# Retention's gate as a transposed product, and one copy moved from ScalarE to VectorE

## The chip, the cores and the metric

One of the eight cores of a Trainium2 chip runs the whole program. The metric is the device time in microseconds of one execution, taken as the median of several runs. The five engines that appear below are TensorE (PE; its weight loads are shown apart, as PEld), VectorE (DVE), ScalarE (ACT), GpSimd (POOL) and SyncE (SP), which here issues nearly all transfers (DMAs). Each engine takes its instructions in the order in which the program emits them.

## The reference

One encoder layer over 1024 tokens of width 1024, all in float32. What matters here is the first half, up to the output projection:

```python
proj = h @ W_in            # split into retention q, k, v, gate; S5 input; attention q, k, v
y_ret = retention(...)     # 4 heads of 64; per head normalised, then multiplied by silu(gate)
y_ssm = s5_mixer(...)      # y = gelu(..); y * sigmoid(y @ w_glu + b_glu)
y_att = window_sink_attention(...)
mix = concatenate([y_ret, y_ssm, y_att]) @ W_out
h = LN(alpha*h + mix); h = LN(alpha*h + ExpertChoiceSwiGLU(h))   # 16 experts, 128 tokens each
```

The last step of retention is the one that is touched: `out = ((out - mu) * rsqrt(var + eps)).reshape(seq, 256)` and `silu(g) * out`, with `g = h @ W_in[:, 768:1024]`. In the state space part it is the turned copy of `y` that feeds the product with `w_glu`.

## The kernel before

Float32 products of full accuracy are made as three products of a split pair: each operand is kept as a high part and a low part (`whl`, `hT`, both of type fp32r), and `mm3` (lines 64 to 66) issues high by high, high by low and low by high. Splitting is a copy on ScalarE (the high part) and a subtraction on VectorE (the low part).

After the input norm the kernel works through a list of products over the projected columns. The order is written out by hand in `order` (line 1237), and each entry advances a place `s`; every piece of work is given a place with `at(place, fn)`, and `F.run()` emits all of it sorted by place. So the places decide the order on each engine's own queue, and on SP's; when an instruction runs is decided by what it waits for. Places below are given relative to `V0`, the place of the first entry.

The entries are:

- `q` (lines 1243 to 1258): attention's queries, eight products `qUH` (column unit U, token half H), transposed, that is columns by 512 tokens, 24 matmuls of 512 columns each in three parts. ScalarE copies the high part to `kst` (line 901), VectorE makes the low part from the same bank (line 936), and SP stores both to `q_d` with four DMAs (line 947).
- `g` (lines 1259 to 1264): retention's gate, one product for each of the eight chunks of 128 tokens, tokens by 256 columns, 24 matmuls of 256 columns in two parts, then Silu on ScalarE into a 256-wide tile (line 403).
- `r` (lines 1265 to 1277): a chunk of retention: scores (line 422) and their decay on VectorE (428), the output (434, 435), statistics on VectorE and GpSimd (442 to 448), the norm (453 on VectorE, 456 on ScalarE), multiplication by the gate on VectorE (460), two transposes on PE (466), a copy out of PSUM on ScalarE (473) and the store to `y_d` on SP (474). The last four stand 4, 6, 9 and 14 behind the output in place; for the last chunk closer.
- `V0 o0 K0 V1 K1`: attention's values and keys, and between them the first output product `o0` of the state space part, which reads what SP loaded into `MUW` (lines 837 to 841) and `Z` (848).

Beside these run other things on the same queues. On VectorE: the scan of the state space part (lines 716 to 719, 724 to 727) and its corrections (`fix`, 742 and 743). On ScalarE: the stores' preparation `SO` (753 to 755), whose last one stands at place 74.75. At place 75.7 `early_space` closes the scan's memory and opens another pool in it: GpSimd and VectorE make `rel` and `R` there (1432 to 1436), and SP issues `sink` and the first eight `MUW` loads; at 81.7 the two loads of `Z` for `o0`. `mat.load(0)` (line 960), the first megabyte of the output matrix, stands at the place of the entry `q30`. Eight small lag products (line 785) lie among the first entries, and their banks are emptied by ScalarE (794); they share two PSUM banks with the scores. The products of the list share two other banks.

After `K1` come the other three output products of the state space part, their turn (`turned`, lines 872 to 879: four copies `yT`, two on ScalarE and two on VectorE), the gate products with `w_glu` (884), attention and the output projection, placed by a table of numbers (`PLACES`, lines 1742 to 1797); then the 16 experts, which are matmuls on split weights loaded a megabyte at a time, from about 455 us to the end.

## Time and profile before

| | |
|---|---|
| median of 3 runs | 1563.07 us (1562.83 to 1563.98) |
| the profiled execution | 1562.62 us, its span 1560.9 us |
| mean granted clock of TensorE | 0.996 |
| busy share of the span | PE 99%, PEld 81%, DVE 90%, ACT 72%, POOL 12% |
| DMA | 507.20 MB, mean 325 GB/s |
| HBM read and written | 461.75 MB and 42.99 MB |

Times in the trace are microseconds from the start of the span. The profiled execution took 1.7 us more than its span. A row of the timeline has the start, the duration, the engine, the line, the operation, the tiles (written <- read) and the shape; in brackets stands the engine's idle time before it and what ended it. A row of the waits has the total, the number of times and the longest. A row of the windows has the busy time of each engine in a stretch, the clock, the share of the DMA engines' time and GB/s.

### The profile page before, as it was taken

What the parts mean: (1) busy time and instruction counts of PE and PEld (TensorE: products, weight loads), DVE (VectorE), ACT (ScalarE), POOL (GpSimd) and SP (SyncE); (2) the same over time, 40 slices, a digit from 0 to 9 for tenths busy, and PEclk for the clock granted to TensorE, in tenths of its full rate; (3) what the DMA queues carried; (4) which work ended last, traced back from release to release, by engine and by line L of the source; (5) the groups of instructions that cost most, each with busy time, mean ns of one, the idle gap of its engine ahead of it and who ended that gap; (6) DMA issues with size and microseconds to landing.
All of it is one profiled execution on the core that took longest, in us unless ns stands there. A gap on an engine that the chain in (4) does not pass through costs nothing.

```text
span 1560.9 us, 21150 instructions
## 1 busy us (share of the span) xinstructions
PE 1543.1 (99%) x7710; PEld 1262.5 (81%) x7710; DVE 1401.8 (90%) x1720; ACT 1130.7 (72%) x1329; POOL 191.5 (12%) x248
## 2 busy tenths in 40 slices
PE   9999999999999999999999999999999999999997
PEld 7887887888767888888888888888888888888886
DVE  7987965889989999999999999989999999999996
ACT  7746556887736777777777777787877878787773
POOL 4002111111010001010010101000211201021121
PEclk9999999999999999999999999999999999999999
DMA  6556478353179999999999999999999999999992
GB/s 242 185 167 155 119 232 234 102 166 109 72 311 371 373 390 411 427 387 367 392 371 387 371 401 370 403 411 409 421 412 409 415 425 413 417 414 413 402 415 108
DMA packets 105177, 507.20 MB, mean 325 GB/s; under 512 B 16752, under 2 KB 29808, under 8 KB 54640
## 3 DMA queue, kind: packets, MB, share of 16 engines
q1 hardware_dynamic: 88624, 474.81, 77.6%
q0 software_dynamic: 16304, 30.94, 7.2%
q8 instruction: 61, 1.00, 0.2%
q14 instruction: 44, 0.36, 0.1%
q10 hardware_dynamic: 144, 0.09, 0.0%
HBM read 461.75 MB, written 42.99 MB: 323 GB/s over the span
## 4 chain that ended last, share of the span: by engine, by line
PE 90%; ACT 3%; DMA 3%; DVE 2%; issue 1%; POOL 1%; SPq 1%; POOLq 0%; ACTq 0%; DVEq 0%
PE gu L2334 44%; PE y L2334 22%; PE mm L64 4%; PE mm L66 4%; PE mm L65 4%; PE tp L2317 3%; PE gu L2342 1%; PE po L1525 1%; PE tp L1505 1%; DMA wraw<-in_w_out 1%; PE at L1454 1%; PE sm L265 0%; DMA uT<-in_x 0%; ACT S L1497 0%; PE at L699 0%
## 5 line engine op out<-in xcount | busy, mean ns | idle before, releaser
L2426 DVE TENSOR_TENSOR whl<-wraw,whl 128x2048 fp32r<-128x2048 f32 x378 | 860.5, 2288 | 61.1 <-ACT whl L2417 57.1
L2417 ACT ACTIVATE whl<-wraw 128x2048 fp32r<-128x2048 f32 x378 | 725.3, 1919 | 246.3 <-PE gu L2334 132.5
L2334 PE MATMUL gu<-whl,xT 128*128 128x512 f32 x3000 | 712.5, 394 | 0.0
L2334 PEld LDWEIGHTS gu<-whl,xT 128*128 128x128 f32 x3000 | 555.4, 188 | 114.8 <-issue 1.0
L2334 PE MATMUL y<-whl,hT 128*128 128x512 f32 x1536 | 359.4, 389 | 0.0
L2334 PEld LDWEIGHTS y<-whl,hT 128*128 128x128 f32 x1536 | 288.0, 188 | 59.7
L2295 POOL DMA_INDIRECT xs<-h_d,index x15 | 26.7, 1777 | 451.3 <-PE y L2334 304.1
L64 PE MATMUL mm<-hT,whl 128*128 128x512 f32 x160 | 65.3, 408 | 0.0
L66 PE MATMUL mm<-hT,whl 128*128 128x512 f32 x160 | 62.6, 391 | 0.0
L65 PE MATMUL mm<-hT,whl 128*128 128x512 f32 x160 | 62.5, 391 | 0.0
L64 PE MATMUL mm<-WO,yh 128*128 128x512 f32 x128 | 53.4, 418 | 0.0
L56 DVE TENSOR_TENSOR hT<-tp,hT 128x512 fp32r<-128x512 f32 x76 | 51.5, 683 | 1.9 <-ACT hT L55 1.7
L55 ACT ACTIVATE hT<-tp 128x512 fp32r<-128x512 f32 x76 | 43.7, 581 | 12.8 <-PE tp L206 6.7
L66 PE MATMUL mm<-WO,yl 128*128 128x512 f32 x128 | 50.6, 396 | 0.0
L65 PE MATMUL mm<-WO,yh 128*128 128x512 f32 x128 | 50.6, 395 | 0.0
L2468 DVE TENSOR_TENSOR hid<-hid,gu 128x512 f32<-128x512 f32 x64 | 43.5, 680 | 2.0 <-PE gu L2334 2.0
L64 PE MATMUL mm<-whl,hT 128*128 128x256 f32 (+1 forms) x120 | 42.4, 353 | 1.5 <-ACT gate L403 1.5
L2462 ACT ACTIVATE hid<-gu 128x512 f32<-128x512 f32 x64 | 37.1, 580 | 5.7 <-PE gu L2342 5.5
L66 PE MATMUL mm<-whl,hT 128*128 128x256 f32 (+1 forms) x120 | 40.2, 335 | 0.0
L65 PE MATMUL mm<-whl,hT 128*128 128x256 f32 (+1 forms) x120 | 40.0, 333 | 0.0
L1465 DVE CUSTOM_DVE_ANT_0 S<-at,R,sink 128x384 f32<-128x384 f32 (+1 forms) x64 | 36.8, 577 | 2.3 <-PE at L1454 1.7
L2317 PEld LDWEIGHTS tp<-ident,hid 128*128 128x128 f32 x256 | 31.8, 140 | 8.5 <-issue 0.5
(450 smaller groups left out, 1779.4 us busy)
## 6 DMA issues: line engine op xcount, KB each, us to landing
wraw<-in_exp_w_up SPq DMA_DIRECT2D x128, 1024.0 KB, 9.5
wraw<-in_exp_w_down SPq DMA_DIRECT2D x128, 1024.0 KB, 10.2
wraw<-in_exp_w_gate SPq DMA_DIRECT2D x122, 1024.0 KB, 9.2
wraw<-in_w_in SPq DMA_DIRECT2D x6, 1024.0 KB, 5.3
whole<-in_exp_w_gate SPq DMA_DIRECT2D x6, 1024.0 KB, 8.5
q_d<-kst SPq DMA_DIRECT2D x32, 128.0 KB, 2.6
wraw<-in_w_out SPq DMA_DIRECT2D x4, 1024.0 KB, 7.6
qs<-q_d POOLq DMA_DIRECT2D x16, 256.0 KB, 3.4
```

Source lines behind the costliest of these rows:

```text
L55: nc.scalar.activation(hi, src, AF.Copy)
L56: eng.tensor_tensor(lo, src, hi.bitcast(F32), OP.subtract)
L64: nc.tensor.matmul(ps, a[0], b[0], start=start, stop=False)
L65: nc.tensor.matmul(ps, a[0], b[1], start=False, stop=False)
L66: nc.tensor.matmul(ps, a[1], b[0], start=False, stop=stop)
L1465: K.nc.vector.tensor_tensor_reduce(S[g][:, :W], K.at.pop((i, g))[:, :W], K.R[:, ro:ro + W], 2.0 ** -(h + 1), K.sink[:, h:h + 1], OP.add, O ...
L2317: K.nc.tensor.transpose(pt[:, c, :], src[:, (c0 + c) * P:(c0 + c + 1) * P], K.ident)
L2334: nc.tensor.matmul(ps, a[s][c], u[:, t, i * w:(i + 1) * w], start=first and id(ps) not in began, stop=last and left[id(ps)] == 0)
L2417: self.K.nc.scalar.activation(u[:, 0, :], self.raw[k1].rearrange("p a b -> p (a b)"), AF.Copy)
L2426: self.K.nc.vector.tensor_tensor(u[:, 1, :], raw, u[:, 0, :].bitcast(F32), OP.subtract)
L2462: nc.scalar.activation(self.h[q], self.pg[q][0], AF.Silu)
L2468: at(self.after, q, 3, lambda: nc.vector.tensor_tensor(self.h[q], self.h[q], self.pg[q][1], OP.mult))
```

## The change

The gate is made transposed. A new class `Gates` makes four products instead of eight, one for each half of the gate's columns and each half of the tokens: gate columns by 512 tokens, 24 matmuls of 512 columns in three parts. Silu goes from PSUM to one tile for each token half, 128 x 2 x 512. The multiplication by the gate is no longer made on the rows: it is made while the turned rows are copied out of PSUM, so that VectorE does `store` with one multiplication where ScalarE made a copy. `gated` is gone. The order of the entries is written anew, norm, turn and store stand 4, 8 and 10 behind the output, and of `yT` VectorE makes all four copies. One place of the table (the low part of the last slice of the output matrix) moves from -8.213 to -7.700.

```diff
--- before.py
+++ after.py
@@ -380,6 +380,27 @@
     K.nc.scalar.activation(K.QT[:, m, half * 512:(half + 1) * 512], p.ps, AF.Copy)
 
 
+class Gates:
+
+
+    def __init__(self, K, units, m, half):
+        self.K, self.units, self.m, self.half = K, units, m, half
+
+    def part(self, c0, c1):
+        K = self.K
+        if c0 == 0:
+            self.ps = K.pmm.tile([P, 512], F32, name="mm")
+        for c in range(c0, c1):
+            mm3(K.nc, self.ps, cols(self.units.u, c, 4, 256, self.m * P, self.m * P + P),
+                [K.hT[s][self.half][:, c, :] for s in range(2)], c == 0, c == KC - 1)
+
+    def put(self):
+        K = self.K
+        if self.m == 0:
+            K.gT[self.half] = K.retB.tile([P, 2, 512], F32, name="gate", bufs=1)
+        K.nc.scalar.activation(K.gT[self.half][:, self.m, :], self.ps, AF.Silu)
+
+
 class Chunk:
 
 
@@ -389,18 +410,6 @@
     def load(self):
         self.kv = self.K.retB.tile([P, 2, 256], F32, name="kv", bufs=3)
         self.K.nc.sync.dma_start(self.kv, self.K.kv_dram[self.t])
-
-    def gate_part(self, units, c0, c1):
-        K, (half, ts) = self.K, token_slice(self.t)
-        if c0 == 0:
-            self.pg = K.pmm.tile([P, 512], F32, name="mm")
-        for c in range(c0, c1):
-            mm3(K.nc, self.pg[:, 0:256], [K.hT[s][half][:, c, ts] for s in range(2)], cols(units.u, c, 4, 256, 0, 256),
-                c == 0, c == KC - 1)
-
-    def gate(self):
-        self.g = self.K.retB.tile([P, 256], F32, name="gate", bufs=3)
-        self.K.nc.scalar.activation(self.g, self.pg[:, 0:256], AF.Silu)
 
     def queries(self):
         K = self.K
@@ -455,10 +464,6 @@
         for h in range(4):
             nc.scalar.activation(self.o[:, h, :], self.po[:, h, :], AF.Identity, bias=nm[:, h:h + 1], scale=self.rs[:, h:h + 1])
 
-    def gated(self):
-        of = self.o.rearrange("p a b -> p (a b)")
-        self.K.nc.vector.tensor_tensor(of, of, self.g, OP.mult)
-
     def turn(self):
         of = self.o.rearrange("p a b -> p (a b)")
         self.pt = self.K.ptp.tile([P, 4, P], F32, name="tp")
@@ -470,7 +475,8 @@
             oT = self.K.ast.tile([P, 2, P], F32, name="roT", tag="k4", bufs=3)
         else:
             oT = self.K.retB.tile([P, 2, P], F32, name="roT", bufs=2)
-        self.K.nc.scalar.activation(oT, self.pt[:, 0:2, :], AF.Copy)
+        half, ts = token_slice(self.t)
+        self.K.nc.vector.tensor_tensor(oT, self.pt[:, 0:2, :], self.K.gT[half][:, :, ts], OP.mult)
         self.K.nc.sync.dma_start(self.K.y_dram[self.t], oT)
 
 
@@ -873,10 +879,7 @@
         if self.yT is None:
             self.yT = self.pool.tile([P, 2, 8, P], F32, name="yT", tag="muw", bufs=1)
         dst, pt = self.yT[:, m, q * 4:q * 4 + 4, :], self.pt.pop((m, q))
-        if q:
-            self.K.nc.vector.tensor_scalar(dst, pt, 0.5, None, op0=OP.mult)
-        else:
-            self.K.nc.scalar.activation(dst, pt, AF.Copy, scale=0.5)
+        self.K.nc.vector.tensor_scalar(dst, pt, 0.5, None, op0=OP.mult)
 
     def gate(self, m, q):
         pg = self.pg[m, q] = self.K.pmm.tile([P, 4, P], F32, name="mm")
@@ -1234,7 +1237,8 @@
     at(V0 - 0.9, lambda: X.update(retB=pool("retB", side="right")))
     at(V0 - 0.8, lambda: setattr(K, "retB", X["retB"][1]))
     chunk = [Chunk(K, t) for t in range(NT)]
-    order = "q00 g0 g1 q01 r0 q10 r1 g2 r2 g3 q11 r3 q20 g4 r4 g5 q21 r5 g6 r6 q30 g7 r7 q31 V0 o0 K0 V1 K1".split()
+    order = "q00 g00 q01 r0 g10 r1 q10 r2 q11 r3 q20 g01 r4 g11 r5 q21 r6 q30 r7 q31 V0 o0 K0 V1 K1".split()
+    K.gT = {}
     s = V0
     unit = {"K": (WA, 0), "V": (WA, 1), "q0": (W6, 0), "q1": (W6, 1), "q2": (W7, 0), "q3": (W7, 1)}
     where = {}
@@ -1257,11 +1261,10 @@
                 at(s + 1.8, lambda w=w, u=u: attention_query(K, X[w], u))
                 at(s + (2.9 if w == "q31" else 1.8), lambda w=w, u=u, half=half: attention_query_store(K, X[w], u, half))
         elif w[0] == "g":
-            c = chunk[int(w[1])]
-            for i in range(2):
-                at(s + i * 1.4, lambda c=c, i=i: c.gate_part(WG, i * 4, i * 4 + 4))
-            s += 2.8
-            at(s + 0.1, c.gate)
+            p = Gates(K, WG, int(w[1]), int(w[2]))
+            thirds(s, p, 1.9)
+            s += 5.6
+            at(s + 0.1, p.put)
         elif w[0] == "r":
             c = chunk[int(w[1])]
             at(s - 17, c.load)
@@ -1272,8 +1275,7 @@
             at(s, c.out)
             s += 2.9
             at(s, c.stats)
-            for gap, fn in zip((2.2, 3.0, 3.78, 4.5) if c.t == NT - 1 else (4, 6, 9, 14),
-                               (c.norm, c.gated, c.turn, c.store)):
+            for gap, fn in zip((2.2, 3.0, 3.9) if c.t == NT - 1 else (4, 8, 10), (c.norm, c.turn, c.store)):
                 at(s + gap, fn)
         else:
             k = qs[int(w[1])]
@@ -1793,7 +1795,7 @@
         "FS": ((-4.644, 0.431), (-2.758, -7.630)),
         "FM": ((-3.768, 4.014), (-2.756, -7.628)),
         "FH": (-19.682, -19.678, 4.258, -15.540),
-        "FL": (-19.680, -19.676, 14.308, -8.213),
+        "FL": (-19.680, -19.676, 14.308, -7.700),
 }
```

## The prediction

> **What bounds the kernel now.** I read the page's busy shares first, then who waited for whom on TensorE between 125 and 290 us, the windows of the stages around the change, and then the timelines and the chain for the places that the change touches.
>
> ```profile
> PE 1543.1 (99%) x7710; PEld 1262.5 (81%) x7710; DVE 1401.8 (90%) x1720; ACT 1130.7 (72%) x1329; POOL 191.5 (12%) x248
> ...
> PE mm L64 <- ACT gate L403: 1.5, 1, 1.5
> PE mm L884 <- ACT yT L879: 0.7, 1, 0.7
> PE po L1525 <- DVE yl L1539: 0.5, 1, 0.5
> ...
> 143.00:183.00 40.00, 40.00 (x268) 34.90 (x268) 37.80 (x133) 16.86 (x41) 8.45 (x12) 1.00 0.61 156
> 183.00:212.00 29.00, 29.00 (x202) 25.46 (x201) 26.84 (x65) 19.48 (x43) 3.50 (x4) 1.00 0.53 146
> 225.00:246.00 21.00, 21.00 (x108) 17.84 (x107) 8.05 (x10) 10.01 (x13) 2.00 (x3) 1.00 0.95 293
> 262.00:280.00 18.00, 16.95 (x69) 10.45 (x68) 14.67 (x37) 17.93 (x50) 3.65 (x17) 1.00 0.32 80
> 280.00:440.00 160.00, 158.40 (x953) 129.92 (x953) 142.32 (x374) 118.96 (x300) 21.45 (x53) 1.00 0.37 118
> ```
>
> TensorE is the bound nearly everywhere, and it hardly waits: the three waits shown make 2.7 us. So a microsecond that TensorE loses at any place reaches the end, and one that it gains is kept only if nothing else arrives later. Behind TensorE stand three others, each in its own stage. VectorE is busy for 64.6 of the 69 us from 143 to 212. From 225 to 246 the DMA engines are 0.95 busy at 293 GB/s, where they were 0.53 busy at 146 GB/s just before. From 262 to 280 ScalarE works 17.93 of 18 us.
>
> **The gate products.** First the pace of TensorE in both shapes: the first and the last of eleven 256-column matmuls in a row, of twenty-one with 512 columns, and two at the start of a run.
>
> ```profile
> 139.29 0.28 PE L65 MATMUL mm<-whl,hT 128*128 128x256 f32 x1
> ...
> 140.48 0.28 PE L66 MATMUL mm<-whl,hT 128*128 128x256 f32 x1
> ...
> 147.10 0.40 PE L64 MATMUL mm<-hT,whl 128*128 128x512 f32 x1
> ...
> 151.65 0.39 PE L66 MATMUL mm<-hT,whl 128*128 128x512 f32 x1
> ...
> 135.17 0.50 PE L64 MATMUL mm<-hT,whl 128*128 128x512 f32 x1
> ...
> 135.50 0.40 PE L65 MATMUL mm<-hT,whl 128*128 128x512 f32 x1
> ```
>
> 1.19 us over ten gives 119 ns for 256 columns, 4.55 over twenty 228 ns for 512. Removed are 8 x 24 x 0.119 = 22.8 us, added 4 x 24 x 0.228 = 21.9: a gain of 0.9. The first matmul of a run, behind work of another form, holds the next up for 0.33 instead of 0.23, so each run costs 0.1 more. Sorting the places by hand gives 27 runs from q00 to K1 now and 19 after the change (the outputs, scores and turns of neighbouring chunks fall together): a gain of 0.8.
>
> [...]
>
> **The first waits.** Silu's table is loaded, then the Silu of g0 frees the bank that g1 needs, and TensorE waited 1.5 us for it.
>
> ```profile
> 140.69 0.41 PE L785 MATMUL at<-WO,BX 128*16 128x128 f32 x8
> ...
> 140.86 1.28 ACT L403 ACT_TABLE_LOAD   x1
> ...
> 142.44 1.10 ACT L794 ACTIVATE KC<-at 16x128 f32<-16x128 f32 x4
> ```
>
> After the change g00 runs 5.5 us, q01 takes the other bank, and the table is loaded under g00: the 1.5 us go. But the last lag product (place 8.2) and the first scores (8.8), between which twelve gate matmuls stood, now stand together. The scores need both of the banks that they share with the lags, and ScalarE needs 1.10 us to empty the last one, of which the first half of the scores hides little. I take 1.0 us of new wait; the ends are 0, if ScalarE is early, and 1.5, the wait that it replaces. The two halves' Silu (four of 512 columns for eight of 256) and the copies that leave ScalarE are off TensorE's path, since ScalarE works 16.9 of 40 us there. On VectorE the eight multiplications move from rows to turned rows and stay as many and as wide. So TensorE gains 0.9 + 0.8 + 1.5 - 1.0 = 2.2 us up to r7.
>
> **Where the lead goes: r6 and r7.** VectorE and ScalarE carry the norms of the last chunks behind the scan's corrections.
>
> ```profile
> 187.47 0.43 DVE L460 TENSOR_TENSOR ro<-ro,gate 128x256 f32<-128x256 f32 x1 [1.36 <-ACT ro L456]
> ...
> 202.47 0.74 DVE L936 SCALAR_TENSOR_TENSOR kst<-mm,qscale,kst 128x512 fp32r<-128x512 f32 x1
> 203.13 1.22 DVE L128 TENSOR_TENSOR whl<-wraw,whl 128x1024 fp32r<-128x1024 f32 x1
> ...
> 209.90 0.16 DVE L453 SCALAR_TENSOR_TENSOR rnm<-rmv,rrs 128x4 f32<-128x4 f32 x1
> ...
> 211.36 1.96 ACT L754 ACTIVATE SO<-VS 128x960 f32<-128x960 f32 x1
> ...
> 214.16 0.56 DVE L1436 TENSOR_TENSOR R<-rel 128x384 f32<-128x384 f32 x1
> ...
> 216.45 0.33 PE L434 MATMUL sm<-kv,sT 128*128 128x64 f32 x2
> ...
> 218.18 0.39 PE L466 MATMUL tp<-ident,ro 128*128 128x128 f32 x2
> ...
> 218.38 0.62 DVE L442 BATCH_NORM_STATS2 rst<-sm 128x6 f32<-128x64 f32 x4 [0.83 <-PE sm L435]
> ...
> 220.73 0.16 DVE L453 SCALAR_TENSOR_TENSOR rnm<-rmv,rrs 128x4 f32<-128x4 f32 x1 [1.25 <-POOL rrs L448]
> ...
> 220.93 1.29 ACT L456 ACTIVATE ro<-sm,rnm,rrs 128x64 f32<-128x64 f32 x4 [3.62 <-DVE rnm L453]
> ...
> 222.83 0.41 PE L466 MATMUL tp<-ident,ro 128*128 128x128 f32 x2
> ```
>
> r5's norm (209.90) comes about 1.7 us earlier: the low parts of q21 and of WA leave from ahead of it (0.74 + 1.22), and so do VectorE's waits for the multiplication by the gate (1.36 here); against that two stores come in, and a wait of about 1.4 us for r5's scores, which stand behind a longer gate product. So 208.2. Behind it ScalarE now has q21's high part and WA's (some 1.7 us) before the last SO (2.2 with its small pieces), which ends at about 213.4, as now; and R, which takes SO's memory, at about 214. Now the point: q21 and r6 have moved back. WA's low part (75.8) and r6's statistics (76.3) stand behind R (75.7), where r6's stood ahead of it. So: 214.0 + 1.2 for WA, statistics from 215.2, and from these to the norm's first number 2.35 (218.38 to 220.73), 217.6, then 1.3 on ScalarE: r6 is ready to be turned at 219.0. TensorE turns it now at 218.18, and after the change it is there at about 216.5, right behind r7's output (216.45 less 2.2, plus 1.8): it waits, and goes on 0.8 later than now. r7's statistics come behind q30's low part, which waits for ScalarE behind r6's norm: 219.0 + 0.7 + 0.75, then 2.35 and 1.3, 224.1 against 222.83 now. So TensorE comes to V0 about 1.3 us late where it could have been 2.2 early. By the ends: VectorE may be 3 us ahead rather than 1.7 (no new waits, TensorE still 0.5 early), or not ahead at all (2.5 late).
>
> **SP's queue.** What SP issues when, and the first product that needs `Z`:
>
> ```profile
> 202.86 3.07 SPq L947 DMA_DIRECT2D q_d<-kst  x4
> ...
> 208.77 0.63 SPq L960 DMA_DIRECT2D wraw<-in_w_out  x1
> ...
> 215.41 0.87 SPq L837 DMA_DIRECT2D MUW<-m_d  x1
> ...
> 223.79 0.99 SPq L848 DMA_DIRECT2D Z<-s_d  x2
> ...
> DMA to landing us min/median/max: 4.8/4.8/4.8
> ...
> 230.15 0.61 PE L859 MATMUL mm<-MUW,Z 128*128 128x128 f32 x4
> ```
>
> With q21 its four stores move from 66.7 to 75.2, between the last SO store and `early_space`: 3.07 us of SP's time that used to lie at 202.86, so that the first MUW load goes out at about 217.4, 2.0 later. With q30, `mat.load(0)` moves from 73.5 to 76.3: from ahead of the MUW loads, where the DMA engines were half idle, to behind them, ahead of `Z` (81.7), while q30's stores (0.5 MB) go behind `Z`. Z lands now at 229.2 (issued 224.4, 4.8 us), and the first matmul that needs it starts at 230.15: 0.9 us to spare. The changed order puts 0.6 MB more ahead of it, some 2 us at the 293 GB/s of this stage. Of the 4 us in all I take 3.1, since the queue starts less filled: Z at 232.3, o0 2.2 us later than now. The ends are 230 (SP no later, the large load beside the small ones) and 233.5.
>
> [...] If the megabyte did not stand in the way, only the 2.0 us of SP would be left, and Z would land at 231.2; no run so far shows this load there.
>
> **What ends last at 280.** The chain that ended last runs through these:
>
> ```profile
> 234.30 5.28 DMA bg<-in_ssm_b_glu
> ...
> 246.72 13.69 DMA wraw<-in_w_out
> ...
> 264.88 0.48 ACT yT L879
> ...
> 265.46 0.46 ACT yT L879
> ```
>
> SP's later transfers follow one another; the bias (`bg`) lands at 239.6, and VectorE waits for it ahead of the keys' low parts, on which the output matrix's parts, their buffer and the last load of the matrix (issued 246.72, landed 260.4) hang in turn. If all of SP's work is 3.3 us later here, this load lands at 263.7, and ScalarE, which waits for it, begins its full stretch that much later; the ends are 0 (the DMA engines catch up) and 4.6. From that stretch the two copies go: 0.48 + 0.46 = 0.94 us. VectorE takes them with about 0.7 each, and is idle for 3.3 of these 18 us, so they cost nothing as long as they lie there; without that room they would cost 1.4. The moved low part (-7.700) only lets them go first. Together 3.3 - 0.94 = 2.4 us later, and TensorE, 2.2 late from o0, is held up by it: it waits for just this chain at 280 already (the 0.5 at `yl`). After 280 it is busy for 158.4 of 160 us, so the 2.4 reach the end.
>
> **The sum.** 1562.62 of the profiled execution + 2.4 = 1565.0. That execution is 0.45 below the median of the runs, 1563.07, so the median should be 1565.5. A measurement of this kernel can tell about 0.2%, 3.1 us, from no change.
>
> **The rivals.**
> - The lead is kept (faster). If Z lands before TensorE comes (about 228) and r6 is turned without a wait, the 2.2 us survive to 246; then the chain at 280 gives its 0.94 alone, or, if the last load goes out 2.2 earlier too, all of 2.2 + 0.94 = 3.1. That is 1560.0 to 1562.1. Decisive is whether SP's loads go out before 215.4. For it speaks that r5's norm comes earlier; against it, the four stores ahead of them.
> - SP's queue costs more: the whole 4.6 us stay in the last load, less 0.94, or VectorE's copies push the `yl` chain too (1.4): 3.7 to 5, 1566.8 to 1568. The 0.95 busy DMA engines speak for it; against it, that large packets move faster than the mix.
> [...]
>
> **How the numbers follow.** Lead given back, 1 to 3 us slower: 0.45, its own range 1563.6 to 1566.2. Lead kept: 0.28, of which 0.08 by more than 3.1. SP costs more: 0.24, nearly all over 3.1. Better pace: 0.03. So faster 0.11, same 0.63, slower 0.26. The range 1560.6 to 1568.0 leaves out the better pace, the best of the kept lead and what lies over 5 us.
>
> **What would show it.** Right: 512-column gate matmuls 228 ns apart; no wait at g's Silu, and one of about 1 us at the first scores; TensorE waiting for r6's norm before q31, and for Z at o0; the last `in_w_out` landing at 262 or later; no `yT` on ScalarE. Wrong: MUW loads issued before 215, o0 starting before 230, or the last load landing by 260, each of which says that the lead was kept.

## The result, and the profile after

The changed kernel takes 1571.88 us (median of 6 runs, 1569.30 to 1573.57) where the kernel before took 1563.84 beside it: a ratio of 1.0052, with a 95% interval of 1.0039 to 1.0065. That is 8.0 us slower (6.1 to 10.2 by the interval). Later it stood again beside the kernel before, at 1.0043 (1.0029 to 1.0057). The profiled execution took 1572.02 us, its span 1570.3.

From the page's busy shares and from who waited for whom on TensorE up to 300 us, in the changed kernel (for waits: engine, tile and line, who ended the wait, us in total, times, longest):

```profile
PE 1545.6 (98%) x7614; PEld 1258.6 (80%) x7614; DVE 1402.0 (89%) x1722; ACT 1126.6 (72%) x1315; POOL 195.3 (12%) x248
...
PE tp L471 <- ACT ro L465: 1.7, 4, 1.0
PE at L1456 <- DVE asm L1467: 1.6, 1, 1.6
PE mm L887 <- DVE yT L882: 1.1, 1, 1.1
PE tp L927 <- ACT va L920: 0.9, 1, 0.9
...
PE at L431 <- ACT KC L800: 0.6, 1, 0.6
```

The wait for `gate` is gone, as the change intended. New are the waits at the turns of retention's rows (`ro`), at the first scores of retention (`KC`) and at V1 (`va`); longer are those at attention's scores (`asm`, 0.2 us before) and for `yT` (0.7 before). Busy time and number of instructions say little: TensorE is busy 2.5 us longer than before with 96 matmuls fewer.

Times of two executions can be set side by side only from a common mark. The first lag product stands ahead of everything that the change touches. The row in the kernel before, and then in the changed one:

```profile
125.03 0.41 PE L785 MATMUL at<-WO,BX 128*16 128x128 f32 x8
```

```profile
126.32 0.41 PE L791 MATMUL at<-WO,BX 128*16 128x128 f32 x8
```

It came 1.3 us later; in the second profile of the same changed kernel 2.8 later, and in the seventeen other kernels of this study between 0.6 earlier and 2.4 later. These differences arise in the first 31 us of the program, in work that is the same in all these kernels, and stay the same from there to the mark. So they are taken as chance and taken off in the table: starts of the same work in the timelines, against the kernel before, counted from this mark.

| later than before by (us) | changed | changed, second profile | early load | SP restored | lead restored | lead, bias moved |
|---|---|---|---|---|---|---|
| r7's output starts | -1.1 | -1.1 | -1.1 | -1.2 | -2.7 | -2.7 |
| r7's turn | +1.8 | +0.5 | +1.9 | +0.1 | -2.7 | -2.7 |
| o0's first matmul with `Z` | +1.7 | +1.8 | +1.8 | +0.6 | -2.2 | -2.2 |
| V1's turn | +3.2 | +4.3 | +1.8 | +0.6 | -0.1 | -1.5 |
| first output product (274 us) | +5.8 | +3.5 | +1.9 | +0.9 | -0.4 | -0.7 |
| last output product (436 us) | +7.2 | +4.1 | +2.0 | +0.8 | +0.2 | -0.9 |
| first expert matmul | +7.9 | +4.3 | +2.9 | +1.7 | +1.0 | +0.1 |
| last matmul | +8.1 | +4.6 | +2.9 | +1.8 | +1.9 | +0.1 |
| first MUW load issued | +2.7 | +2.7 | +2.7 | -0.2 | -1.7 | -1.7 |
| second pair of `Z` issued | +4.1 | +4.3 | +1.8 | +0.3 | -0.3 | -0.3 |

(The four columns on the right are the experiments e1, e8, e14 and e17. The "first output product" and the "last output product" belong to the projection with `W_out`; the times in brackets are those of the kernel before.) Three stretches carry the loss. TensorE has a lead at r7 and loses it in the next few microseconds:

```profile
143.64 0.71 PE L431 MATMUL at<-QT,kv 64*128 64x128 f32 x4
144.94 0.71 PE L431 MATMUL at<-QT,kv 64*128 64x128 f32 x4 [0.59 <-ACT KC L800]
...
163.30 0.33 PE L471 MATMUL tp<-ident,ro 128*128 128x128 f32 x1 [0.17 <-ACT ro L465]
163.90 0.33 PE L471 MATMUL tp<-ident,ro 128*128 128x128 f32 x1 [0.27 <-ACT ro L465]
...
219.54 0.33 PE L471 MATMUL tp<-ident,ro 128*128 128x128 f32 x1 [1.02 <-ACT ro L465]
220.14 0.47 PE L471 MATMUL tp<-ident,ro 128*128 128x128 f32 x1 [0.27 <-ACT ro L465]
220.26 0.77 PE L64 MATMUL mm<-hT,whl 128*128 128x512 f32 x1
220.83 0.63 PE L65 MATMUL mm<-hT,whl 128*128 128x512 f32 x1
221.26 0.63 PE L66 MATMUL mm<-hT,whl 128*128 128x512 f32 x1
```

This is TensorE's timeline of the changed kernel; in brackets stands the idle time before an instruction and what ended it. The rows at 163 us are the turn of r0, those at 219.5 the turn of r6. After the turn of r6 the 512-column matmuls follow at 0.43 us and not at 0.23. The windows of the same profile show why (the third number from the end is the granted clock): 0.56 of full speed.

```profile
219.50:223.40 3.90, 3.59 (x10) 2.73 (x11) 2.06 (x11) 1.16 (x3) 0.77 (x1) 0.56 0.67 177
```

The windows of the stages that were shown of before, each moved by the lateness of its start, are much the same in the changed kernel: VectorE is busy for 63.7 of 69 us, the DMA engines 0.94 at 326 GB/s, ScalarE 17.3 of 18 us. The loss is in waits between them, not in a fuller engine:

```profile
144.00:184.00 40.00, 38.97 (x224) 32.67 (x222) 36.59 (x127) 17.23 (x40) 7.80 (x12) 1.00 0.61 152
184.00:213.00 29.00, 28.89 (x173) 24.48 (x173) 27.11 (x64) 18.89 (x40) 5.49 (x5) 1.00 0.49 123
...
227.00:250.00 23.00, 22.45 (x112) 18.59 (x111) 7.07 (x9) 9.82 (x13) 2.01 (x3) 1.00 0.94 326
...
269.00:287.00 18.00, 16.49 (x65) 9.85 (x63) 14.76 (x38) 17.29 (x48) 2.96 (x17) 1.00 0.27 75
```

The second stretch is SP's queue. In the kernel before, SP's last stores of retention and the second pair of `Z` went out without the large load ahead of them:

```profile
225.22 1.68 SPq L474 DMA_DIRECT2D y_d<-roT  x3
229.97 0.80 SPq L848 DMA_DIRECT2D Z<-s_d  x2
```

SP's waits, and then its timeline, in the changed kernel:

```profile
SPq L763 <- ACT SO L761: 10.2, 2, 7.3
...
SPq L854 <- DMA y_d<-roT: 2.3, 1, 2.3
SPq L480 <- DMA wraw<-in_w_out: 1.9, 1, 1.9
...
215.76 2.98 SPq L950 DMA_DIRECT2D q_d<-kst  x4
...
219.41 0.45 SPq L843 DMA_DIRECT2D MUW<-m_d  x1
...
223.55 0.78 SPq L963 DMA_DIRECT2D wraw<-in_w_out  x1
224.43 0.38 SPq L480 DMA_DIRECT2D y_d<-roT  x1
225.76 1.05 SPq L854 DMA_DIRECT2D Z<-s_d  x2
227.19 2.87 SPq L950 DMA_DIRECT2D q_d<-kst  x4
232.03 0.80 SPq L480 DMA_DIRECT2D y_d<-roT  x2
235.34 0.80 SPq L854 DMA_DIRECT2D Z<-s_d  x2
...
238.55 0.43 SPq L832 DMA_DIRECT2D bg<-in_ssm_b_glu  x1
```

Count from the large load at 223.55: it, r5's store, two `Z` and four stores of queries make eight transfers, and the ninth, r6's store (`y_d` at 232.03, with r7's right behind it), does not go out until the large load has landed, at 231.96; SP's wait of 1.9 us is put down to just that load. In the trace SP's 618 transfers are counted on eight semaphores in turn, without a break, and none goes out before the one eight places ahead of it is done. So here one megabyte among smaller transfers holds up what stands eight places behind it. The second pair of `Z` then waits until r6's store has landed (2.3 us), and goes out 4.1 us late, counted from the mark; behind it the bias goes out 3.0 and the last load of the matrix 3.7 us late.

The third stretch is what waits for those loads. VectorE, ScalarE and TensorE in the changed kernel, in order of time:

```profile
244.68 0.17 DVE L835 TENSOR_SCALAR hb<-bg 128x2 f32<-128x2 f32 x1 [6.70 <-DMA bg<-in_ssm_b_glu]
244.75 0.68 DVE L56 TENSOR_TENSOR KHL<-mm,KHL 64x512 fp32r<-64x512 f32 x1
...
245.46 0.60 ACT L55 ACTIVATE KHL<-mm 64x512 fp32r<-64x512 f32 x1 [2.72 <-DVE KHL L56]
...
249.88 0.60 ACT L920 ACTIVATE va<-mm 128x512 f32<-128x512 f32 x1
...
250.53 0.66 PE L927 MATMUL tp<-ident,va 128*128 128x128 f32 x4 [0.94 <-ACT va L920]
...
267.53 1.06 ACT L970 ACTIVATE WO<-wraw 128x1024 fp32r<-128x1024 f32 x1 [3.25 <-DMA wraw<-in_w_out]
...
272.10 0.16 DVE L1492 TENSOR_TENSOR asm<-asm 128x4 f32<-128x4 f32 x1 [2.77 <-ACT asm L1480]
...
272.39 0.66 DVE L882 TENSOR_SCALAR yT<-tp 128x512 f32<-128x512 f32 x1
```

VectorE stands idle 6.7 us for the bias (5.1 in the kernel before), and behind it stand the keys' low parts; ScalarE waits for these (2.72), V1's rows (`va`) stand behind that on ScalarE, and TensorE waits for them (0.94). ScalarE starts on the last load of the matrix at 267.53 (260.44 before). The fourth `yT` copy stands on VectorE behind its wait of 2.77 us for ScalarE's sums.

### The profile page after: what moved, and what is told of

Its sections match the earlier page's. It is cut to its first block, busy times and chain, and to the rows that moved or that the text cites. A ratio compares the mean times of both kernels' runs of the same rounds, so it can differ in the third digit from the quotient of the medians.

```text
span 1570.3 us, 20944 instructions
## 1 busy us (share of the span) xinstructions
PE 1545.6 (98%) x7614; PEld 1258.6 (80%) x7614; DVE 1402.0 (89%) x1722; ACT 1126.6 (72%) x1315; POOL 195.3 (12%) x248
## 4 chain that ended last, share of the span: by engine, by line
PE 85%; DMA 6%; DVE 4%; ACT 3%; issue 1%; POOL 1%; SPq 0%; POOLq 0%; ACTq 0%; DVEq 0%
PE gu L2336 43%; PE y L2336 21%; PE mm L64 4%; PE mm L66 4%; PE mm L65 4%; PE tp L2319 3%; DMA wraw<-in_w_out 2%; PE gu L2344 1%; PE po L1527 1%; PE tp L1507 1%; PE at L1456 1%; DMA wraw<-in_exp_w_down 1%; DMA acc_d<-ah 1%; DMA wraw<-in_exp_w_gate 1%; DMA uT<-in_x 1%
## 5 line engine op out<-in xcount | busy, mean ns | idle before, releaser
L64 PE MATMUL mm<-hT,whl 128*128 128x512 f32 x192 | 78.8, 410 | 0.0
L66 PE MATMUL mm<-hT,whl 128*128 128x512 f32 x192 | 75.5, 393 | 0.0
L65 PE MATMUL mm<-hT,whl 128*128 128x512 f32 x192 | 75.4, 393 | 0.0
L64 PEld LDWEIGHTS mm<-hT,whl 128*128 128x128 f32 x192 | 36.7, 191 | 8.5 <-issue 1.5
L66 PEld LDWEIGHTS mm<-hT,whl 128*128 128x128 f32 x192 | 36.3, 189 | 8.2 <-DVE whl L128 0.2
L65 PEld LDWEIGHTS mm<-hT,whl 128*128 128x128 f32 x192 | 36.6, 191 | 6.6
```

Source lines behind the costliest of these rows:

```text
L64: nc.tensor.matmul(ps, a[0], b[0], start=start, stop=False)
L65: nc.tensor.matmul(ps, a[0], b[1], start=False, stop=False)
L66: nc.tensor.matmul(ps, a[1], b[0], start=False, stop=stop)
```

## The experiments

Of each run the ratio to the kernel before, measured beside it, is given with its 95% interval.

**e1_load_early.** The first load of the output matrix goes out ahead of the last SO stores.

```diff
-    at(where["q30"], lambda: mat.load(0))
+    at(where["q30"] - 1.6, lambda: mat.load(0))
```

> The changed kernel with one thing undone: the first load of the output matrix (1 MB) is issued ahead of the last SO stores again, as before, and not between the MUW loads and Z. In the changed kernel the last two retention stores (y_d) waited on SP for that load until 232.0, and the second Z, the next MUW loads, the bias and the last loads of the matrix, which follow on SP, went out 5.4 us late (235.3 for 230.0). Queue theory: with the load gone from there, the retention stores go out at about 229, the second Z at about 232.5, the bias lands near 241.7 instead of 244.6, the last in_w_out at about 264.7 instead of 267.5, and the kernel is 2 to 3.5 us faster than the changed one: 1568.5 to 1570. Bandwidth theory (the bytes have to move anyway, and the prediction's 2 us for Z were the whole effect): Z of o0 comes 2 us earlier, the last load by less than 1, and the time stays within 1 us, 1571 to 1572.5. TensorE theory (what TensorE loses at r6's turn, wait and half clock, is what counts): no change, 1571.9.

Measured: 1.0021 (1.0011 to 1.0030), 1566.21 us. SP's timeline of this run:

```profile
208.05 0.63 SPq L963 DMA_DIRECT2D wraw<-in_w_out  x1
...
220.10 0.44 SPq L843 DMA_DIRECT2D MUW<-m_d  x1
...
230.58 0.81 SPq L480 DMA_DIRECT2D y_d<-roT  x2
233.79 0.80 SPq L854 DMA_DIRECT2D Z<-s_d  x2
```

The mark came 0.7 us later than in the changed kernel's profile, and still r6's store goes out 1.4 us and `Z` 1.6 us earlier on the clock, the last load lands 3.1 earlier (264.39). One place in SP's queue was worth 0.2 to 0.3% (3.4 to 4.8 us, against 1.0043 and 1.0052), at or above the upper end of the queue theory's 2 to 3.5 us, and the bandwidth and TensorE theories, which gave 1 us or nothing, are out: TensorE's losses at r6 are all still there (+1.9 at r7's turn), and o0 starts on `Z` no sooner (+1.8), although its first pair lands 2.2 us earlier. So what counted came behind that pair.

**e2_turn_late.** r6's turn goes behind nine matmuls of q31.

```diff
-            for gap, fn in zip((2.2, 3.0, 3.9) if c.t == NT - 1 else (4, 8, 10), (c.norm, c.turn, c.store)):
+            for gap, fn in zip((2.2, 3.0, 3.9) if c.t == NT - 1 else (4, 10.2, 11.2) if c.t == 6 else (4, 8, 10), (c.norm, c.turn, c.store)):
```

> The changed kernel with r6's turn placed 2.2 later (10.2 instead of 8 behind its statistics, its store 11.2), so that TensorE does nine matmuls of q31 first. It takes away the wait for r6's norm (1.3 us) and, if the half clock from 220.3 to 223.4 (granted clock 0.56) comes from that wait, another 1.3 us. Queue theory: V0 starts 2.0 to 2.6 us earlier, but o0 then waits for Z, which still lands at 233.6, and the chain at 280 is as late as it was: 1571 to 1572. TensorE theory: the 2.6 us stay until the end, 1569.3. If the clock does not drop for that wait but for another cause, the slow stretch is seen again and V0 gains 1.3 at most.

Measured: 1.0042 (1.0029 to 1.0055), no clear difference from the changed kernel. A miss in part: r6's turn no longer waits, but r7's does, and the half clock comes there (0.59 from 223.0 to 227.2):

```profile
222.96 0.33 PE L471 MATMUL tp<-ident,ro 128*128 128x128 f32 x1 [1.63 <-ACT ro L465]
```

r7's norm hangs on r6's through VectorE and ScalarE, so moving one turn only moves the wait.

**e3_order.** q21 ahead of r5.

```diff
-    ... r4 g11 r5 q21 r6 q30 ...
+    ... r4 g11 q21 r5 r6 q30 ...
```

> The changed kernel with q21 ahead of r5 (order: ... r4 g11 q21 r5 r6 q30 ...): q21's four stores and WA's low part go out 2.9 earlier, ahead of the last SO stores and of R. Queue theory: SO ends about 1.5 us earlier on ScalarE, R too, r6's statistics start about 2 us earlier, so TensorE finds r6 normed and neither waits nor slows (2.6 us earlier at V0); the MUW loads go out near 216 instead of 219.4, and all of SP's queue behind them, with the large load still in it, comes about 3 us earlier: 1568 to 1569.5. Rival: r6 right behind r5 on VectorE delays r5 or r6, and the wait moves there: no gain, 1571 to 1573.

Measured: 1.0046 (1.0033 to 1.0059). The rival held: TensorE now waits 4.8 us for r5 and comes to V0 7.4 us later than before, 5.7 later than in the changed kernel. And the time is the same. So when TensorE reaches V0 does not decide the time by itself. The edit does not take the two theories apart, though: it also lets SP go earlier (the first MUW load by 2.0 us, counted from the mark).

**e4_yt_alone** and **e12_before_yt_early.** The kernel before with the second part of the change alone (all `yT` on VectorE, low part at -7.700); the second also takes the fourth copy and its transposes ahead of VectorE's wait for the sums.

```diff
-        "FT": ((-10.699, -15.320), (-8.793, -12.470)),
-        "FC": ((-9.800), (-8.001)),
+        "FT": ((-10.699, -15.320), (-9.900, -12.470)),
+        "FC": ((-9.800), (-9.620)),
```

> The kernel before with the second part of the change alone: all four yT copies on VectorE and the low part's place -7.700; gates as before. The prediction gave it -0.94 us at 280 (1562.9 from 1563.8). In the changed kernel the fourth yT copy stood behind VectorE's wait of 2.77 us for the sum of the exponentials, and the matrix's low part behind it, and YO came 0.26 us earlier counted from the last load, while the path of TensorE from the first scores to YO took 0.84 us longer. So the first theory is -0.3 to 0 (1563.5 to 1563.8); the rival is +0.8, a new wait that replaces the old (1564.6).

> The kernel before (gates in rows) with all four yT copies on VectorE and the fourth ahead of the wait for the sums. With the fourth behind that wait the ratio was 1.0003 (0.9994 to 1.0012). If the lost place was all that stood against the prediction's 0.94 us, the ratio is 0.9994 here (0.9 us faster); if not, 1.0000.

Measured: 1.0003 (0.9994 to 1.0012) and 1.0005 (0.9996 to 1.0015). No gain can be seen in either, and 0.94 us (0.9994) is at or outside the ends. The rows of the kernel before (ScalarE's start on the last load of the matrix and its second copy), then of the first of these two kernels (VectorE's fourth copy; ScalarE had begun on that load at 260.55):

```profile
260.44 1.06 ACT L967 ACTIVATE WO<-wraw 128x1024 fp32r<-128x1024 f32 x1 [0.77 <-DMA wraw<-in_w_out]
...
265.37 0.57 ACT L879 ACTIVATE yT<-tp 128x512 f32<-128x512 f32 x1
```

```profile
265.40 0.66 DVE L876 TENSOR_SCALAR yT<-tp 128x512 f32<-128x512 f32 x1
```

The fourth copy starts 4.9 us after ScalarE begins on that load, whichever engine makes it (272.39 less 267.53 in the changed kernel as well). And the first output product follows ScalarE's start on that load by 13.38 us in the kernel before, by 13.36 in e4 and in the changed kernel: the copies that left ScalarE were worth 0.02 us there and not 0.94. With the fourth copy ahead of the wait it is 13.14 (e12), and that 0.2 does not show in the time.

**e5_again.** The changed kernel, unaltered.

> The changed kernel once more, unaltered, to stand beside the other runs of this call. From the first time it should be 0.39 to 0.65% above the kernel before, 1571.9 where that is at 1563.8. TensorE's first 130 us, which the change leaves as they were, began 1.2 us later in the changed kernel's profile than in that of before; if this is chance, the mark moves by about a microsecond either way here, and if it belongs to the change it is 1.2 again.

Measured: 1.0043 (1.0029 to 1.0057), 1570.07 us. Its profile is the second column of the table. r6's turn waits as in the first profile, but the clock holds:

```profile
221.01 0.33 PE L471 MATMUL tp<-ident,ro 128*128 128x128 f32 x1 [1.01 <-ACT ro L465]
```

```profile
221.00:225.00 4.00, 3.72 (x16) 2.94 (x17) 2.06 (x11) 1.13 (x3) 0.90 (x1) 1.00 0.67 169
```

And TensorE, 1.3 us earlier at r7's turn for it, then waits 0.8 us for `Z`: at the first matmul with `Z` both executions are level (+1.7 and +1.8).

**e6_wa_low** and **e7_load_wa.** WA's low part behind r6's statistics, alone (shown) and with the early load of e1.

```diff
-            at(where[name] + 8.0, lambda wt=wt, i=i: wt.low(i))
+            at(where[name] + (9.4 if name == "q21" else 8.0), lambda wt=wt, i=i: wt.low(i))
```

> The changed kernel with WA's low part (1.2 us on VectorE) behind r6's statistics and not ahead of them, where it can run while GpSimd makes the root. The prediction's third step said that R and this part stand ahead of r6's statistics and hold up its norm. If so, r6 is ready to be turned about 1.1 us earlier, the wait of 1.0 + 0.3 us at its turn falls to 0.2 or less and the granted clock stays at 1.00 between 219.5 and 223.4 (0.56 in the changed kernel): V0 starts 2.3 us earlier, unless r7's turn takes the wait over, as in the kernel with r6's turn placed later. Queue theory: with SP's queue as late as it was, the end gains less than 1.5 us. TensorE theory: 2.3 us at the end. If R alone is the cause, the wait stays at 1 us.

> Both: the first load of the output matrix ahead of the last SO stores and WA's low part behind r6's statistics. The early load alone was at 1.0021 of the kernel before, with r6's wait of 1.3 us and the slow clock still in it. If the two losses add, this one is 2.3 us faster than that, at about 1.0007 (1564.0 where before is at 1562.9). If SP's queue still sets the end (the MUW loads go out at 219.4 to 220.1, behind q21's stores, against 215.4 before), TensorE waits at Z or at 280 instead and the gain is under 1 us: 1.0018.

Measured: 1.0042 (1.0028 to 1.0056) and 1.0028 (1.0017 to 1.0038). r6's turn comes 0.4 us earlier rather than 1.1, no half clock follows (1.00 from 215 to 225 in e6, 0.23 us between matmuls in e7), TensorE meets `Z` (1.1 us of wait in the first), and nothing is left at the end. The two losses do not add: the second is not faster than the early load alone.

**e8_load_wa_store.** As e7, and q21's low part and its four stores ahead of the last SO stores.

```diff
-                at(s + 1.8, lambda w=w, u=u: attention_query(K, X[w], u))
+                at(s + (1.2 if w == "q21" else 1.8), lambda w=w, u=u: attention_query(K, X[w], u))
-                at(s + (2.9 if w == "q31" else 1.8), ...
+                at(s + (2.9 if w == "q31" else 1.3 if w == "q21" else 1.8), ...
```

> As the one before, and q21's four stores go out ahead of the last SO stores, for which SP waited 6.6 us (208.7 to 215.3) in the kernel with the early load, and no longer behind them; q21's low part on VectorE goes 0.6 earlier for it. The MUW loads should go out 2.7 to 3 us earlier, at about 216.5, the first Z land by 230 and the last in_w_out by 262. If SP's queue sets the end, the kernel gains 2 to 3 us on the one before and is 1 to 2 us faster than the kernel before the change (0.999); if TensorE's own time at r6 and r7 sets it, there is no difference between the two.

Measured: 1.0015 (1.0006 to 1.0024). SP is where it was in the kernel before (first MUW load 0.2 earlier, second `Z` 0.3 later), and the last load lands 0.9 late. The kernel is some 2 us faster than e7, as the queue theory had it, though the intervals overlap; the expected lead over the kernel before the change isn't there.

**e9_stats, e10_yt_early, e11_both.** On e8: r6's statistics ahead of R (shown); the fourth `yT` early, as in e12; both.

```diff
-            at(s, c.stats)
+            at(s - (0.65 if c.t == 6 else 0), c.stats)
```

> The kernel with the early load, WA's low part later and q21's stores ahead of the last SO stores (1.0015 of before), and r6's statistics also ahead of R, which on VectorE waits for ScalarE's SO. With WA's low part out of the way r6's turn came only 0.4 us earlier and still waited 0.7 + 0.3 us, so by the prediction's third step R must hold most of it: r6's statistics start about 2 us earlier, the waits at the turns of r6 and r7 go down to 0.3 each or less, and V0 starts 0.7 to 1.5 us earlier. If TensorE's time sets the end, that much reaches it: 1.0008. Queue theory: SP's queue is the same, Z and the last in_w_out land at the same times, and nothing of it is left at the end: 1.0015.

> The same kernel as the base of the one before (1.0015), r6 untouched, but the fourth yT copy and the transposes that it reads placed ahead of VectorE's wait for the exponentials' sums. In every profile with the copies on VectorE the fourth one ends 5.4 us after ScalarE begins on the last matrix part, as ScalarE's copy did in the kernel before (260.44 to 265.85; 267.53 to 272.97 in the changed one), so the 0.94 us that the prediction took from ScalarE's chain were lost to VectorE's queue. If so, glu and the first output product now come 0.7 to 1 us earlier against the landing of the last in_w_out, and the kernel is at 1.0009. Rival: the scores, the sums or the landing itself set the first output product, and it stays at 1.0015.

> Both of the edits before together. If each counts for itself: 1.0002 or below. Queue theory: the yT copy alone counts, 1.0009.

Measured: 1.0023 (1.0014 to 1.0032), 1.0019 (1.0010 to 1.0027), 1.0020 (1.0012 to 1.0029): no gain in any. In e9 the root on GpSimd now stands ahead of R's iota, and R, ahead of the norm's last number, waits for it on VectorE:

```profile
215.13 0.36 DVE L1435 TENSOR_SCALAR rel<-rel 128x384 f32<-128x384 f32 x1 [1.64 <-POOL rel L1434]
```

In e10 VectorE no longer makes a copy behind the sums, but ScalarE then waits 1.07 us for TensorE's first product with `wg`, and the first output product follows ScalarE's start on the last load by 13.75 us instead of 13.36; what holds that product up stays open.

**e13_norm** and **e14_lead.** On e8: r6's statistics and its norm both ahead of R. Then also the first scores behind 15 of the gate's and queries' matmuls, and r0's to r5's turns and r0's to r6's stores 1.0 later.

```diff
-            at(s, c.stats)
+            at(s - (0.65 if c.t == 6 else 0), c.stats)
...
-                at(s + gap, fn)
+                at(s - 0.62 if c.t == 6 and gap == 4 else s + gap, fn)
...
-            at(s - 8, c.scores)
-            at(s - 7, c.decayed)
+            at(s - (8 if c.t else 5.5), c.scores)
+            at(s - (7 if c.t else 4.5), c.decayed)
...
-            for gap, fn in zip((2.2, 3.0, 3.9) if c.t == NT - 1 else (4, 8, 10), (c.norm, c.turn, c.store)):
+            for gap, fn in zip((2.2, 3.0, 3.9) if c.t == NT - 1 else (4, 8 + (c.t < 6), 11), (c.norm, c.turn, c.store)):
```

> The kernel with the early load, WA's low part later and q21's stores first (1.0015), with r6's statistics and the last number of its norm ahead of R on VectorE, so that r6's norm waits neither for SO nor for the iota of R on GpSimd; in the kernel with the statistics alone moved, the norm's last number stayed behind R, which then waited 1.64 us for that iota, and r6's turn came 0.8 us later instead of earlier. Now r6's norm should be ready near 216.2 and r6's turn wait for nothing, r7's norm come about 1 us earlier, and V0 start 1.5 to 2.6 us earlier. TensorE theory: that much reaches the end, 1.0000 to 1.0005. Queue theory: TensorE meets Z or the chain at 280 and less than 1 us of it is left: 1.0010 to 1.0015.

> The kernel of the run before, and two more of TensorE's waits taken away: the first scores stand behind the first 15 matmuls of the gate and query products instead of right behind the last lag product (1.53 us there), and the turns of r0 to r5 stand 1.0 later (r1's turn waited 0.87 us). r7's output should start 2 us earlier. TensorE theory: 1.5 to 2.4 us more at the end than the run before, 0.9985 to 0.9995. Queue theory: TensorE waits for Z or at 280, no difference between the two.

Measured: 1.0030 (1.0018 to 1.0042) and 1.0012 (1.0003 to 1.0021). The first is above what either theory allowed (1.0015 at most), and neither is clear of e8 (1.0015). At V0 the edits do what was meant: r6's turn waits for nothing, the granted clock over the two executions is 0.998 and 0.997, and TensorE is 0.7 and 2.2 us earlier than in the kernel before. At V1's turn it is 1.4 later and 0.1 earlier: the lead is gone. VectorE's row in e14 shows a place where it goes; ScalarE's keys wait behind it (3.68 us, 0.75 in e17 below):

```profile
240.49 0.17 DVE L835 TENSOR_SCALAR hb<-bg 128x2 f32<-128x2 f32 x1 [7.63 <-DMA bg<-in_ssm_b_glu]
```

**e15_yt_back** and **e16_gates_alone.** The `yT` copies and the low part as before the change, on e8 and on the changed kernel.

```diff
-        self.K.nc.vector.tensor_scalar(dst, pt, 0.5, None, op0=OP.mult)
+        self.K.nc.vector.tensor_scalar(dst, pt, 0.5, None, op0=OP.mult) if q else self.K.nc.scalar.activation(dst, pt, AF.Copy, scale=0.5)
```

> The kernel with the early load, WA's low part later and q21's stores first (1.0015), with the two yT copies on ScalarE and the matrix's low part at -8.213 as before the change. In all profiles the fourth copy ended 5.4 us after ScalarE began on the last part of the matrix, on either engine. So no difference is expected: 1.0010 to 1.0020. If the prediction was right that ScalarE's chain gains 0.94 from it, this one is 1.0021; if the copies on VectorE cost something, 1.0008 or less.

> The first part of the change alone: gates transposed, in the changed kernel's order, with the yT copies and the low part's place as before the change. By the theory that SP's queue and TensorE's waits at r6 make the whole loss, it is as slow as the changed kernel: 1.0043 to 1.0052. If the yT copies have a part in the loss, it is below 1.0040.

Measured: 1.0022 (1.0013 to 1.0031) and 1.0053 (1.0040 to 1.0066). 1.0022 is the number that was named for the case that the copies gain 0.94 us, but 1.0015, e8's own, lies in its interval as well, so the times of e8 and e15 do not decide. The traces do: from ScalarE's start on the last load to the first output product it is 13.38 us with two copies on ScalarE (e15, e16, the kernel before) and 13.36 with all four on VectorE (e8, the changed kernel). The gates alone cost what the whole change costs.

**e17_lead_bias** and **e18_before_bias.** The bias's instruction on VectorE moved from behind K0 to behind V1, in e14 and in the kernel before.

```diff
-    at(where["K0"] + 1.0, out.bias)
+    at(where["V1"] + 2.2, out.bias)
```

> The kernel with TensorE's waits at the first scores, r6 and r7 taken away and SP's order restored (1.0012), with the bias's instruction on VectorE (hb) moved from behind K0 to behind V1, where its load has long landed. If hb's wait of 7.6 us is what passes SP's lateness on, K0's low parts start near 238 instead of 240.6, TensorE does not wait at V1 (1.3 us for va), V1 is reached 2 us earlier than in the kernel before, the loads 4 and 6 of the output matrix go out some 2 us earlier, and the kernel is 1 to 2 us faster than the run before: 0.9999 to 1.0006. If the loads of the output matrix are held by SP's ring or by the DMA engines anyway, the last in_w_out lands as before and the gain is under 0.5: 1.0010 to 1.0012.

> The kernel before with hb moved in the same way. There K0's low part waited at most 0.4 us for hb (ScalarE's part ended at 239.3, hb at 239.8), so 0 to -0.4 us: 0.9997 to 1.0000.

Measured: 1.0004 (0.9995 to 1.0013) and 1.0003 (0.9994 to 1.0012). VectorE in e17 no longer waits for the bias there, and starts on the keys 2.9 us earlier than in e14, counted from the mark (there 240.57):

```profile
236.96 0.68 DVE L56 TENSOR_TENSOR KHL<-mm,KHL 64x512 fp32r<-64x512 f32 x1 [4.77 <-ACT KHL L55]
```

V1's turn is 1.5 us earlier than in the kernel before, the first output product 0.7. This is the fastest kernel with the transposed gates, level with the kernel before, which no kernel of this study beats. Against e14 the gain is not clear of the noise, since the intervals overlap. In the kernel before the same move changes nothing, as was expected. What takes the rest of the lead (0.9 at the last output product) shows among TensorE's waits in e17 behind that product:

```profile
PE tp L2185 <- DMA z<-h_d,cindex: 1.0, 1, 1.0
```

## Why the prediction was right or wrong

The sign was right, the size was not: 2.4 us were forecast and 6.7 to 8.0 measured, above the range. The rival "SP's queue costs more" came nearest, but it too was priced too low (1566.8 to 1568), and it had the bytes for its cause, not the place in the queue. What it held against itself, that large packets move faster than the mix, the kernel before shows: 397 GB/s at 500 to 520 us, where the experts' weights come in megabytes (1136 packets for 7.93 MB, DMA share 1.01), against 293 at 225 to 246 (3697 for 6.15 MB, 0.95). Where this section gives two numbers, they are those of the changed kernel's two profiles, counted from the mark on the clock of the kernel before; so counted, these are 8.1 and 4.6 us late at the last matmul.

- **The gate's products: right.** By the gaps between starts the 256-column matmuls took 24.4 us and the gate's 512-column ones 22.8, and the queries' products, interrupted less often, took 45.5 instead of 46.5 (second profile): a gain of 2.6, where 0.9 + 0.8 were summed. By these sums a matmul of the gate took 0.24 us with 512 columns and 0.13 with 256: no run shows the better pace, to which 0.03 was given.
- **The first waits: right in place, small in size.** The 1.5 us for Silu are gone. From the first scores to the next product it is now 1.9 us and was 0.65, so that they cost 1.3 more, where 1.0 was taken. Not foreseen: r0's turn now waits for ScalarE's norm (0.17 and 0.27 us of idle time; from the scores' start ahead of it to the next product 1.57, at r1's turn 0.84), and retention's outputs take 0.5 more. The lead at r7 was 1.1 and not 2.2.
- **r6 and r7: right in place.** r6's norm ended at 218.8 in both profiles (said: 219.0), and V0 began 1.7 and 1.0 later than before (said: 1.3). What was missing is the half clock after the wait, which the first profile has and the second hasn't, so that the first number is near by luck. That R and WA's low part hold r6 up is borne out, in unequal parts: with WA's part out of the way 0.4 us were won (e6), and r6 was free only with its statistics and its norm also ahead of R (e13).
- **SP and `Z`: right number.** The first MUW load went out 2.7 later (said: 2.0), the first pair of `Z` had landed at 232.3 and 232.6 (said: 232.3), and o0's first matmul with it came 1.7 and 1.8 later (said: 2.2). Without the megabyte ahead of it 231.2 had been worked out, and the two profiles agree with the later number.
- **What ends last at 280: this step failed, on both its terms.** SP's lateness entered the sum as 3.3 us at the last load, with 4.6 as the end. Measured, VectorE got the bias 3.7 and 4.8 late, SP issued the last load 3.7 and 4.8 late, and ScalarE began on it 5.8 and 3.5 late. So the 3.3 were 2.5 short in one profile and nearly met in the other; the difference lies in how long this load took to land (2.1 us more and 1.3 less than before), and why it took longer or shorter is not shown. The mechanism was incomplete in both. The step saw the megabyte as bytes ahead of `Z`; it did not see that r6's store, eight transfers behind, would wait until it had landed, nor that the second `Z`, the bias and the loads follow that store. e1 shows it by moving the load alone: half of the whole loss or more went (1.0052 and 1.0043 to 1.0021). The other term, 0.94 us for the copies that leave ScalarE, was nothing, 0.02: the fourth copy took a place on VectorE behind a wait for ScalarE, and starts 4.9 us after ScalarE's start on the last load as before (e4, e15, e16). "Idle for 3.3 of these 18 us" was true of VectorE, but that idle time was a wait in order, ahead of the copy.
- **After 280: this failed too, by less.** It was said that the 2.4 reach the end as they are. In fact the changed kernel loses 2.3 and 1.1 more between the first output product and the end. In all sixteen profiles with transposed gates 0.1 to 1.0 us more than in the kernel before go between the last output product and the first expert matmul, in the other three with gates in rows -0.1 to 0.1. The gather of the candidates' rows (`z`) ends that wait in several of them; why it lands later was not tried, and stays open.

The working theory itself had to be mended on the way. The prediction began with "a microsecond that TensorE loses at any place reaches the end", and up to V0 that does not hold: 5.7 us more (e3, where SP went earlier too) changed nothing, 2.8 us less (e8 to e14) little. But neither does SP's queue alone decide: with SP restored (e8) about 2 us were left. In the traces the bias on VectorE leads from the one to the other: with its instruction moved (e17), V1's turn comes 1.4 us earlier than in e14, and with TensorE's lead restored as well the transposed gates are level with the kernel before. For this last step the times alone are no proof (1.0012 and 1.0004, overlapping). So the lead of the transposed gates exists (2.7 us at r7 in e17) and is used up behind it, about 1.2 by V1, 0.8 by the first output product, and the rest by the gather, in the places where something else ends last.

## What to carry to other kernels

When an order of work changes, write out the new order of each DMA queue and count: with a fixed number of transfers in flight (eight on SP here), look at what stands that many places behind each large one (here r6's store, which waited 1.9 us for the megabyte), and who waits for it in order. Moving work to an engine that "has room" gained 0.02 us here and not 0.94, its place in that engine's order being behind a wait of 2.77 us (0.2 with the place ahead of it); read the idle time in brackets before the instruction, not the busy share. And an instruction that waited for a load held up what was queued behind it on its engine (VectorE stood idle 6.70 us for the bias, ahead of the keys' low parts), so put it where its data has long been there.

## What the runs showed of the hardware

- A wait of only 1.0 to 1.6 us on TensorE was followed by about 3 us at half pace: 0.43 us between 512-column matmuls instead of 0.23, granted clock 0.56 in the changed kernel (219.5 to 223.4), 0.59 in e2. The same wait of 1.01 us in the second profile of the same kernel was not (1.00). Over the profiles of this study: behind waits of 1.63 us at r7's turn (e2) and 1.46 at r6's (e9) the half clock came both times (0.59 and 0.64); behind 1.0 it came in two of four (0.56 in the changed kernel, 0.63 in e1; not in the changed kernel's second profile, and e16's whole execution was granted 0.998, as that one was); behind 0.7 in none of five (1.00 in the windows of e6 and e8, 0.23 us between matmuls in e7 and e10, 0.998 over the execution of e15). The stretch lasts 3.41 us in the changed kernel's trace, at 0.5, and worked out from the windows' clocks 3.4 in e2 and e9 as well. In e3, with a wait of 4.8 us, it lasts longer: the 512-column matmuls still stand 0.43 us apart at 228.6 to 229.0, 7.2 us after r5's turn began (221.43). At r6's turn TensorE was idle for 1.3 us in all in both profiles of the changed kernel (1.02 and 0.27, 1.01 and 0.27), and the half clock followed in one of them; what decides it is not shown.
- The start of the program varies by more than the effects under study: the first lag product, ahead of all that was changed, came up to 2.8 us later and up to 0.6 earlier than in the kernel before. Two profiles are compared from a mark behind that.
